# Two plain blocks per FFN in place of four, and weight splits and sinks' exponentials moved in ScalarE's queue

## The chip, the cores and the metric

The kernel runs on one core of a Trainium2 chip. The core has five engines that work side by side: TensorE (PE in the profile; PEld is its weight load), VectorE (DVE), ScalarE (ACT), GpSimd (POOL) and SyncE (SP), which here only issues DMAs. Each takes its instructions in the order in which the compiled program has them. The metric is the device time of one execution in microseconds; lower is better. The time of the kernel before is the median of three runs.

## The reference

What is computed is a decoder trunk of two layers over 512 tokens of width 1024. Each layer is a half-step gated FFN, a mixer, a second half-step FFN and a final norm.

```python
def swiglu(x, w1, w3, w2):
    return (jax.nn.silu(x @ w1) * (x @ w3)) @ w2
...
    for l in range(DEPTH):
        h = x + 0.5 * swiglu(rms_norm(x, ffn1_norm[l]), ffn1_w1[l], ffn1_w3[l], ffn1_w2[l])

        n = rms_norm(h, mix_norm[l])
        p = n @ w_in[l]
        u_conv, q, k, v, q_mem = jnp.split(p, splits, axis=-1)

        y_conv = conv_module(u_conv, conv_w[l], conv_b[l], conv_ln_g[l], conv_ln_b[l])
...
        y_swa = sliding_window_attention(q, k, v, swa_sinks[l])
...
        y_mem = memory_attention(qm, mk, mv)

        y = jnp.concatenate([y_conv, y_swa, y_mem], axis=-1)
        h = h + y @ w_out[l]

        h = h + 0.5 * swiglu(rms_norm(h, ffn2_norm[l]), ffn2_w1[l], ffn2_w3[l], ffn2_w2[l])

        x = rms_norm(h, final_norm[l])
```

The hidden width of an FFN is 2816, 22 blocks of 128. The mixer has 384 channels of a causal depthwise convolution with 31 taps, six heads of attention in a window of 128 with a learned sink each, and four heads that attend to 256 memory tokens. All of it is in float32.

## The kernel before, in words

Every float32 operand of a matmul is split into a rounded high part and a low part that holds the rest (`split`, lines 144 to 146): ScalarE writes the high part, VectorE the low one. A product is then three matmuls, high by high, low by high, high by low (`mm3`, lines 175 to 178). Weights arrive by a DMA into a `raw` tile, of which there are three, and are split into one of four pairs `whi`, `wlo`. For some weights the low part is made without VectorE: ScalarE writes the high part and the negated high part's source (lines 150 and 151), and a DMA on GpSimd's queue adds the weights to it in place (line 152, `split_by_dma`).

**The FFN** (line 405 on). Tokens are in the columns, and x is the residual h times the norm's gain; the factor R of the norm, one per token, comes later, from column sums of squares (`sums`), a small matmul that spreads it over all partitions (`spread`) and a copy by ScalarE. The first four blocks of the hidden width are "plain" (`PLAIN`, line 269): two projections (w1 and w3) of 24 matmuls with 512 columns for each block, run on x, and after that `gate` multiplies by R, applies silu and splits the result. While they run, VectorE makes n = h times gain times R (`normed`) and the operands of a scheme that needs seven products in place of eight for a pair of blocks (`Seven`): `first` makes operands 1, 2 and 6 (`mh`, `ml`), `rest` makes 3, 5, 7 and 4, in the tiles of x, which come free with the last plain projection. From there on `up_pair` (line 341) does two blocks at a time: 14 products of 12 matmuls with 256 columns for both w1 and w3. It splits seven weight tiles on ScalarE and VectorE (`unit`); some of them are sums of two blocks' weights, which DMAs (line 349) and VectorE (line 369) add up. Four quarters of the hidden width follow one another, and at the end of each one w2 is applied and added into h (line 475).

In the layer-1 first FFN, h must also be scaled by the final norm of layer 0 (`after`, line 1050). This is eight VectorE instructions (line 1053), queued behind the first seven-product pair.

How many projections come before the column sums and the spread is given by `at_product`: two and one for the first FFN of a layer, one and one for the second. So behind R there are in the first FFN one, in the second two of the first four projections.

**The mixer** (line 623 on). At the end of an FFN `last(d)` calls `Next`, which rounds the new operand `xhi` on ScalarE (line 155), takes the rest on VectorE (line 156) and squares h on ScalarE (line 236) for the column sums. Then `ORDER` (line 47) says in which order the mixer's steps are written: c are halves of convolution projections, q and Q query and key projections and their transposes, v and V value and memory-query projections and their transposes, g the scores of an attention group, a the rest of the attention, t the conv taps of a channel block, s the conv's norm and the output projection. The four query weight tiles (`queries`, line 693) are split ahead of the first q; three of them by `split_by_dma`.

The conv's taps are 30 VectorE instructions for each of three channel blocks after a first one (lines 932 and 939). `EARLY` of them go freely, and `LATER` deals the others out over the attention groups: a tap may only come after the softmax step `biased` of its group.

In attention (line 861 on), ScalarE makes the exponentials of scores (`powers`, line 800) and copies transposed ones out of PSUM (line 812), TensorE multiplies them with the values (line 821), and `scaled` adds the exponential of the sink (line 829) to the sums. Its argument `esw` comes from GpSimd (line 791). Output weights (`out_weights`, line 920 on) are split by ScalarE and a DMA; two before the attention and two in the midst of it.

The compiler schedules: it orders the instructions of each engine by the order in which they are written and by when it expects them to be ready. `tc.issue_after(i)` adds an edge: what its block writes on the engine of `i` stands behind `i` in that engine's queue. `queued()` is this with the last matmul.

Of the kernel before, what the change touches and what calls it, by code (L numbers as in the profile page):

```python
# [46 lines left out]
ORDER = "c00 c01 q0 c10 q1 c11 Q0 q2 q3 Q1 c20 c21 Q2 v0 v1 V0 Q3 V1 g0 g1 v2 v3 a t0 t1 t2 s"  # L47

EARLY = 49
LATER = (1, 12, 5, 4, 3, 3, 3, 3, 3, 3)  # L50
# [14 lines left out]
def trunk(ctx: ExitStack, tc: tile.TileContext, xT, memT, pos, w1a, w3a, w2a, w1b, w3b, w2b,  # L65
# [88 lines left out]
    def split_scaled(hi, lo, x, col):  # L154
        A.activation(hi, x, AF.Copy, scale=col)
        V.scalar_tensor_tensor(out=lo, in0=x, scalar=col, in1=hi.bitcast(F32), op0=ALU.mult, op1=ALU.subtract)

# [95 lines left out]
    class Next:  # L253
# [5 lines left out]
        def __call__(self, d):  # L259
            split_scaled(self.x[0][:, d, :], self.x[1][:, d, :], h[:, d, :], self.gain[:, d : d + 1])  # L260
            for s, scale in self.stats:
                s.add(h[:, d, :], 1.0 if scale is None else scale[:, d : d + 1])
# [78 lines left out]
    def up_pair(l, w13, f, M):  # L341
# [26 lines left out]
        def add(out, a, b):  # L368
            V.tensor_tensor(out=out, in0=a, in1=b, op=ALU.add)  # L369
# [15 lines left out]
        for i in range(2):  # L385
            w = unit(X[i])
            product(xy[i][:, x0], w, 1, 5)
            A.activation(part[i][:, x0], xy[i][:, x0], AF.Copy)
            product(zv[i][:, x1], w, 0, 7)
            add(to[i][:, :, x1], zv[i].rearrange("p (n t) -> p n t", n=2), part[i][:, x0].unsqueeze(1).to_broadcast([P, 2, QT]))  # L390
# [14 lines left out]
    def ffn(l, w13, w2, x, sums, factors, last, at_product, aside=None):  # L405
# [14 lines left out]

        g, products = {}, []
        for f in range(0, PLAIN, 2):
            g[f], g[f + 1] = gated()
# [16 lines left out]
        with queued():  # L440
            for f in range(0, PLAIN, 2):
                u, v = (tmp.tile([P, 2, S], F32, tag=t, name=t, bufs=n) for t, n in (("u", 1), ("g", 2)))
                for j in range(2):
                    while len(products) < 2 * (f + j) + 2:
                        products.append(up(len(products) // 2, len(products) % 2))
                    gate(products[2 * (f + j) :], R, u[:, j], v[:, j], *g[f + j])
                if not f:
                    M.first()
        M.rest()
        for q, (f0, nf) in enumerate(QUARTERS):  # L450
            ahead = 2 if q + 1 < len(QUARTERS) else 0
            for f in range(f0, f0 + nf + ahead, 2):
                if f not in g:
                    g[f], g[f + 1] = up_pair(l, w13, f, M)
                    if f == PLAIN:
                        with tc.issue_after(M.gated.ins):
                            after()
# [86 lines left out]

    def head_scale(ps, col, n, out=None):

        sq = tm("hsq", "sq", 2)[:, 0 : n * HD]
        A.activation(sq, ps, AF.Square, scale=col)
# [74 lines left out]
    def mixer(l, x, st, last):  # L623
# [69 lines left out]
        def queries(t):  # L693
            if not t:
                ww["q"] = [weights(wqk[l, i], 1024, G if i else V, spare()) for i in range(4)]
# [30 lines left out]
        def values(t):  # L726
# [9 lines left out]
            head_scale(ps[:, 0:256], rc[:, t : t + 1], NM, rm[:, t, :])  # L736

# [85 lines left out]
        def scaled(kind, b, po):  # L823
# [3 lines left out]
            if kind == "w":  # L827
                e = esw[:, b]
                A.activation(e, e, AF.Exp)
# [31 lines left out]
        def attention():  # L861
# [18 lines left out]
            for d in range(2):  # L880
                with tc.issue_after(keyed[2].ins):
                    out_weights(d)
            yy.extend([gated_pair() for _ in range(KD // 2)][::-1])
            y.extend(at(p, ALL, i, ALL) for p in yy for i in range(2))
            for n, (kind, *pairs) in enumerate(GROUPS):
# [8 lines left out]
                if n in (3, 5):  # L894
                    with tc.issue_after(raised[GROUPS[n - 1][0], *GROUPS[n - 1][-1]].ins):
                        out_weights(len(out_w))
# [108 lines left out]
    def stages(st, gain):  # L1005
        def factors(r):
            return gain, kept(spread(r), "R"), lambda: None
# [3 lines left out]
    for l in range(L):  # L1011
# [16 lines left out]
        mixer(l, nxt.x, before, into(gn[:, l, N_FFN2], (st, None)))  # L1028
        sums, factors = stages(st, gn[:, l, N_FFN2])
        st, fin = Stat("st"), gn[:, l, N_FIN]  # L1030
        if l + 1 < L:
# [15 lines left out]
            def factors(r, gg=gg, fin=fin):  # L1047
                R = kept(spread(r[1]), "R")

                def after():  # L1050
                    RF = kept(spread(r[0]), "RL")
                    for d in range(KD):
# [70 lines left out]
```

## Time and profile before

| | |
|---|---|
| time, median of 3 runs (lowest to highest) | 1791.13 us (1789.97 to 1793.52) |
| the profiled execution's own time | 1790.99 us |
| its span | 1789.2 us |
| mean granted TensorE clock | 0.994 |
| TensorE busy | 1757.0 us (98%) |
| VectorE busy | 1272.3 us (71%) |
| ScalarE busy | 899.4 us (50%) |
| GpSimd busy | 194.4 us (11%) |
| DMA | 253.32 MB, mean 142 GB/s |

The span runs from the first to the last instruction of the profiled execution; 1.8 us of its time lie outside. In a row of the timeline stand the start in us, the duration in us, the engine, the line of the kernel, the operation, what it writes and reads by the program's names, and the count; in square brackets the idle time of the engine ahead of it and what ended it. Matmuls overlap: one of 512 columns has a duration of 0.39 us, but the next one starts sooner, so the distance of starts is what a matmul costs. Line 176 is the high-by-high matmul of a product, 177 low by high, 178 high by low.

### The profile page before, as it was taken

The numbers are of one execution on the slowest core, as the hardware profiler recorded it, in microseconds if no ns is written. First come the engines' busy times: TensorE is split into PE (matmuls) and PEld (weight loads), VectorE is DVE, ScalarE is ACT, GpSimd is POOL, SyncE is SP. The second block draws the span as 40 slices with busy tenths as digits, with TensorE's granted clock in tenths as the row PEclk, the third lists the DMA queues.
The fourth block names the chain that finished last, engine by engine and source line by source line (L and its number), as shares of the span: only waits on it lengthen the run. The fifth ranks groups of instructions, "written<-read, shape, count | busy, mean of one in ns | idle before, by whom it ended". The sixth has DMA issues, their size and how long they took to land.

```text
span 1789.2 us, 28081 instructions
## 1 busy us (share of the span) xinstructions
PE 1757.0 (98%) x11004; PEld 1581.5 (88%) x11004; DVE 1272.3 (71%) x1887; ACT 899.4 (50%) x1367; POOL 194.4 (11%) x217
## 2 busy tenths in 40 slices
PE   8999999999999999999999999999999999999997
PEld 6989999878788989898889898989787889998986
DVE  6969666589947857575678685756797567666755
ACT  6646444464765535353655453535455655453532
POOL 1001000034221000000010000000441210000000
PEclk9999999999999999999999999999999999999998
DMA  9456555183167547464656474643631966574622
GB/s 280 125 163 177 165 139 145 57 217 70 30 176 172 139 136 177 127 173 128 165 136 170 131 190 135 169 114 105 158 70 30 234 127 171 136 183 119 168 74 82
DMA packets 95892, 253.32 MB, mean 142 GB/s; under 512 B 9872, under 2 KB 14224, under 8 KB 95760
## 3 DMA queue, kind: packets, MB, share of 16 engines
q1 hardware_dynamic: 77040, 190.45, 34.9%
q0 software_dynamic: 18720, 61.09, 19.3%
q8 instruction: 86, 1.41, 0.3%
q14 instruction: 46, 0.38, 0.1%
HBM read 249.40 MB, written 2.10 MB: 141 GB/s over the span
## 4 chain that ended last, share of the span: by engine, by line
PE 81%; issue 6%; DVE 6%; DMA 4%; ACT 3%; POOL 0%; SPq 0%; POOLq 0%; DVEq 0%; ACTq 0%
PE mm L177 12%; PE mm L176 11%; PE mm L178 11%; PE po L176 8%; PE po L178 8%; PE po L177 8%; PE pt L176 6%; PE pt L177 6%; PE pt L178 6%; DVE there L939 2%; DMA glo<-in_wqk 1%; DMA raw<-in_wout 1%; DVE wlo L146 1%; PE cf L178 1%; PE cf L176 1%
## 5 line engine op out<-in xcount | busy, mean ns | idle before, releaser
L145 ACT ACTIVATE whi<-raw 128x1024 fp32r<-128x1024 f32 (+3 forms) x344 | 324.5, 945 | 440.5 <-PE mm L177 223.5
L146 DVE TENSOR_TENSOR wlo<-raw,whi 128x1024 fp32r<-128x1024 f32 (+3 forms) x344 | 372.0, 1083 | 133.9 <-ACT whi L145 132.6
L177 PE MATMUL mm<-glo,whi 128*128 128x512 f32 x752 | 293.3, 390 | 0.8 <-DVE glo L146 0.8
L176 PE MATMUL mm<-ghi,whi 128*128 128x512 f32 x752 | 293.3, 392 | 0.0
L178 PE MATMUL mm<-ghi,wlo 128*128 128x512 f32 x734 | 285.7, 389 | 0.9 <-DVE wlo L146 0.9
L177 PE MATMUL po<-ml,whi 128*128 128x256 f32 x864 | 244.5, 283 | 0.0
L178 PE MATMUL po<-mh,wlo 128*128 128x256 f32 x864 | 244.5, 283 | 0.0
L176 PE MATMUL po<-mh,whi 128*128 128x256 f32 x864 | 244.4, 283 | 0.0
L176 PE MATMUL pt<-xhi,whi 128*128 128x256 f32 x864 | 243.3, 283 | 0.6 <-DVE g L369 0.6
L178 PE MATMUL pt<-xhi,wlo 128*128 128x256 f32 x864 | 243.9, 283 | 0.0
L177 PE MATMUL pt<-xlo,whi 128*128 128x256 f32 x864 | 243.9, 283 | 0.0
L475 DVE SCALAR_TENSOR_TENSOR h<-mm,h 128x512 f32<-128x512 f32 x128 | 87.8, 689 | 133.3 <-PE mm L178 133.3
L177 PEld LDWEIGHTS mm<-glo,whi 128*128 128x128 f32 x752 | 141.3, 188 | 29.9 <-DVE glo L146 1.6
L176 PEld LDWEIGHTS mm<-ghi,whi 128*128 128x128 f32 x752 | 141.3, 188 | 29.4 <-DVE h L475 1.2
L176 PEld LDWEIGHTS pt<-xhi,whi 128*128 128x128 f32 x864 | 165.2, 192 | 1.7 <-DVE g L369 0.8
L177 PEld LDWEIGHTS pt<-xlo,whi 128*128 128x128 f32 x864 | 165.7, 192 | 0.8
L176 PEld LDWEIGHTS po<-mh,whi 128*128 128x128 f32 x864 | 165.8, 192 | 0.7
L177 PEld LDWEIGHTS po<-ml,whi 128*128 128x128 f32 x864 | 165.8, 192 | 0.6
L178 PEld LDWEIGHTS po<-mh,wlo 128*128 128x128 f32 x864 | 165.8, 192 | 0.0
L178 PEld LDWEIGHTS pt<-xhi,wlo 128*128 128x128 f32 x864 | 165.6, 192 | 0.0
L178 PEld LDWEIGHTS mm<-ghi,wlo 128*128 128x128 f32 x734 | 137.8, 188 | 30.2 <-DVE wlo L146 1.3
L939 DVE SCALAR_TENSOR_TENSOR there<-ypad,par,there 128x512 f32<-128x512 f32 x180 | 136.7, 770 | 1.6
(312 smaller groups left out, 3312.9 us busy)
## 6 DMA issues: line engine op xcount, KB each, us to landing
raw<-in_w2a SPq DMA_DIRECT2D x48, 384.0 KB, 3.5
raw<-in_w2b SPq DMA_DIRECT2D x48, 384.0 KB, 3.6
raw<-in_w1b SPq DMA_DIRECT2D x26, 512.0 KB, 3.7
raw<-in_w3b SPq DMA_DIRECT2D x26, 512.0 KB, 4.1
raw<-in_w1a SPq DMA_DIRECT2D x25, 512.0 KB, 3.7
raw<-in_w3a SPq DMA_DIRECT2D x25, 512.0 KB, 3.8
wsum<-in_w1a SPq DMA_DIRECT2D x18, 512.0 KB, 4.5
wsum<-in_w3a SPq DMA_DIRECT2D x18, 512.0 KB, 4.4
```

The lines of the kernel that those rows point to most:

```text
L145: A.activation(hi, x, AF.Copy)
L146: on.tensor_tensor(out=lo, in0=x, in1=hi.bitcast(F32), op=ALU.subtract)
L176: T.matmul(ps, a[0], b[0], start=first, stop=False, **more)
L177: T.matmul(ps, a[0], b[1], start=False, stop=False, **more)
L178: tail[0] = T.matmul(ps, a[1], b[0], start=False, stop=last, **more)
L475: added = V.scalar_tensor_tensor(out=h[:, d, :], in0=ps, scalar=0.5, in1=h[:, d, :], op0=ALU.mult, op1=ALU.add)
L939: V.scalar_tensor_tensor(out=cv[:, c, :], in0=ypad[:, c, j : j + S], scalar=conv_w[:, c, j : j + 1], in1=cv[:, c, :], op0=ALU.mult, op1=AL ...
```

## The change

`plain` is 4 in the program's first FFN and 2 in the three others. There the third and fourth block are done by `up_pair`, and the final scaling of h in the layer-1 FFN comes in two halves, the first behind the first seven-product pair, the second within the next pair. In the mixer three of the four query weight splits are queued behind the last rounding of x; the third block of values (v2) is written ahead of the first scores; the output weights are split in steps v0 and v2 and no longer in the attention; the sink's exponential is queued behind the last exponentials of its block's scores; and `EARLY` and `LATER` are dealt anew.

```diff
-ORDER = "c00 c01 q0 c10 q1 c11 Q0 q2 q3 Q1 c20 c21 Q2 v0 v1 V0 Q3 V1 g0 g1 v2 v3 a t0 t1 t2 s"
-
-EARLY = 49
-LATER = (1, 12, 5, 4, 3, 3, 3, 3, 3, 3)
+ORDER = "c00 c01 q0 c10 q1 c11 Q0 q2 q3 Q1 c20 c21 Q2 v0 v1 V0 Q3 v2 g0 V1 g1 v3 a t0 t1 t2 s"
+
+EARLY = 55
+LATER = (1, 12, 5, 4, 3, 3, 3, 3, 2, 2)
...
-            split_scaled(self.x[0][:, d, :], self.x[1][:, d, :], h[:, d, :], self.gain[:, d : d + 1])
+            self.rounded = split_scaled(self.x[0][:, d, :], self.x[1][:, d, :], h[:, d, :], self.gain[:, d : d + 1])
...
+        plain = PLAIN if first else 2
         g, products = {}, []
-        for f in range(0, PLAIN, 2):
+        for f in range(0, plain, 2):
             g[f], g[f + 1] = gated()
...
-            for f in range(0, PLAIN, 2):
+            for f in range(0, plain, 2):
...
-                    if f == PLAIN:
-                        with tc.issue_after(M.gated.ins):
-                            after()
+                    if f in (plain, plain + 2):
+                        with tc.issue_after((M.gated if f == plain else M.turned).ins):
+                            after(f > plain)
...
             if not t:
-                ww["q"] = [weights(wqk[l, i], 1024, G if i else V, spare()) for i in range(4)]
+                ww["q"] = []
+                for i in range(4):
+
+                    with tc.issue_after(operand.rounded.ins) if i else nullcontext():
+                        ww["q"].append(weights(wqk[l, i], 1024, G if i else V, spare()))
...
+            for d in {0: (0, 1, 2), 2: (3,)}.get(t, ()):
+                with tc.issue_after((squared[-1] if d > 1 else keyed[2]).ins):
+                    out_weights(d)
...
-                A.activation(e, e, AF.Exp)
+                with tc.issue_after(raised[kind, b, CC - 1].ins):
+                    A.activation(e, e, AF.Exp)
...
-            for d in range(2):
-                with tc.issue_after(keyed[2].ins):
-                    out_weights(d)
...
-                if n in (3, 5):
-                    with tc.issue_after(raised[GROUPS[n - 1][0], *GROUPS[n - 1][-1]].ins):
-                        out_weights(len(out_w))
...
-                def after():
-                    RF = kept(spread(r[0]), "RL")
-                    for d in range(KD):
+                def after(half):
+                    if not half:
+                        spreads.append(kept(spread(r[0]), "RL"))
+                    RF = spreads[0]
+                    for d in range(4 * half, 4 * half + 4):
                         V.scalar_tensor_tensor(out=h[:, d, :], in0=h[:, d, :], scalar=fin[:, d : d + 1], in1=RF, op0=ALU.mult, op1=ALU.mult)
```

`M.turned` is the last addition that takes the sixth and seventh product's results out of PSUM (line 390), `squared[-1]` the latest square for a head's norm (line 548), `keyed[2]` the copy of the third block of keys (line 720), `first` a list that the program's first FFN empties.

More of the change, by code (lines that the diff above doesn't have):

```diff
@@ L154, in split_scaled @@
     def split_scaled(hi, lo, x, col):
-        A.activation(hi, x, AF.Copy, scale=col)
+        rounded = A.activation(hi, x, AF.Copy, scale=col)
         V.scalar_tensor_tensor(out=lo, in0=x, scalar=col, in1=hi.bitcast(F32), op0=ALU.mult, op1=ALU.subtract)
+        return rounded
     def pair():
@@ L368, in add @@
         def add(out, a, b):
-            V.tensor_tensor(out=out, in0=a, in1=b, op=ALU.add)
+            return V.tensor_tensor(out=out, in0=a, in1=b, op=ALU.add)
         for i in range(2):
@@ L389, in up_pair @@
             product(zv[i][:, x1], w, 0, 7)
-            add(to[i][:, :, x1], zv[i].rearrange("p (n t) -> p n t", n=2), part[i][:, x0].unsqueeze(1).to_broadcast([P, 2, QT]))
+            M.turned = add(to[i][:, :, x1], zv[i].rearrange("p (n t) -> p n t", n=2), part[i][:, x0].unsqueeze(1).to_broadcast([P, 2, QT]))
         w = unit(z)
@@ L543, in heads @@
         return x.rearrange("p (h e) -> p h e", e=HD)
+    squared = []
     def head_scale(ps, col, n, out=None):
         sq = tm("hsq", "sq", 2)[:, 0 : n * HD]
-        A.activation(sq, ps, AF.Square, scale=col)
+        squared.append(A.activation(sq, ps, AF.Square, scale=col))
         ss, v = sm(n, f"hs{n}"), sm(n, f"hv{n}")
@@ L621, in prepare, with mixer @@
         memory(l)
-    def mixer(l, x, st, last):
+    def mixer(l, operand, st, last):
+        x = operand.x
         o = CC * TAPS
@@ L1006, in factors @@
         def factors(r):
-            return gain, kept(spread(r), "R"), lambda: None
+            return gain, kept(spread(r), "R"), lambda half: None
         return lambda: rms_cols(st, D), factors
@@ L1027, in trunk @@
         before, st = st, Stat("st")
-        mixer(l, nxt.x, before, into(gn[:, l, N_FFN2], (st, None)))
+        mixer(l, nxt, before, into(gn[:, l, N_FFN2], (st, None)))
         sums, factors = stages(st, gn[:, l, N_FFN2])
@@ L1047, in factors @@
             def factors(r, gg=gg, fin=fin):
-                R = kept(spread(r[1]), "R")
-                def after():
-                    RF = kept(spread(r[0]), "RL")
-                    for d in range(KD):
+                R, spreads = kept(spread(r[1]), "R"), []
+                def after(half):
[3 more added lines that the diff above has]
+                    for d in range(4 * half, 4 * half + 4):
                         V.scalar_tensor_tensor(out=h[:, d, :], in0=h[:, d, :], scalar=fin[:, d : d + 1], in1=RF, op0=ALU.mult, op1=ALU.mult)
```

## The prediction

> **What bounds the kernel now.** I read the page first (busy shares and the chain that ended last), then the busy time of each engine in the stretches that the change touches, then the timelines of those stretches.
>
> ```profile
> span 1789.2 us, 28081 instructions
> ...
> PE 1757.0 (98%) x11004; PEld 1581.5 (88%) x11004; DVE 1272.3 (71%) x1887; ACT 899.4 (50%) x1367; POOL 194.4 (11%) x217
> ...
> PE 81%; issue 6%; DVE 6%; DMA 4%; ACT 3%; POOL 0%; SPq 0%; POOLq 0%; DVEq 0%; ACTq 0%
> ```
>
> TensorE is busy for 98% of the span and makes 81% of the chain. So time is won in two ways only: fewer or shorter matmuls, or one of the few waits of TensorE taken away. Everything else counts only where it makes TensorE wait. The profiled execution took 1790.99 us for its span of 1789.2 us; the median of the runs is 1791.13 us, 0.14 us more, so I sum against the profiled execution and carry the result over unchanged.
>
> The next view is the busy time by engine in six stretches (us, then PE, PEld, DVE, ACT, POOL busy, the granted clock, DMA share, GB/s).
>
> ```profile
> 556.50:587.60 31.10, 31.10 (x139) 25.76 (x138) 26.61 (x39) 14.62 (x20) 2.43 (x3) 1.00 0.57 122
> 910.20:935.80 25.60, 25.60 (x114) 21.21 (x113) 25.53 (x38) 12.52 (x17) 1.49 (x2) 1.00 0.45 100
> ...
> 370.00:390.00 20.00, 19.09 (x90) 14.98 (x89) 12.12 (x20) 13.62 (x17) 5.85 (x6) 1.00 0.89 241
> 430.00:440.00 10.00, 9.19 (x60) 8.62 (x61) 8.98 (x17) 5.34 (x14) 4.32 (x4) 1.00 0.67 133
> ...
> 455.00:460.00 5.00, 3.17 (x30) 2.77 (x27) 4.97 (x10) 4.06 (x12) 2.19 (x4) 1.00 0.00 0
> 460.00:465.00 5.00, 5.00 (x28) 3.46 (x27) 3.99 (x8) 2.50 (x8) 0.91 (x2) 0.66 0.74 131
> ```
>
> The first two rows run, in the second FFN of layer 0 and the first FFN of layer 1, from the moment the row factor R is there to the first matmul of the seven-product scheme. TensorE has no gap in either. VectorE is busy for 26.61 of 31.10 us in the one and 25.53 of 25.60 us in the other: in the layer-1 FFN it is already full under the cover of the plain blocks. The other rows are in the mixer of layer 0. At 455 to 460 us TensorE works only 3.17 of 5 us, and in the 5 us after that its granted clock is 0.66.
>
> **Part 1: two plain blocks in three FFNs.** Four projections of 24 matmuls, 512 columns wide, are replaced by 14 products of 12 matmuls, 256 wide. Their price is the distance between starts on TensorE's timeline.
>
> ```profile
> 571.32 0.39 PE L176 MATMUL mm<-xhi,whi 128*128 128x512 f32 x1
> ...
> 587.63 0.28 PE L176 MATMUL po<-mh,whi 128*128 128x256 f32 x1
> ...
> 593.39 0.40 PE L176 MATMUL pt<-xhi,whi 128*128 128x256 f32 x2
> ```
>
> Three projections (72 matmuls by the code) lie between the first two rows: 16.31/72 = 0.2265 us each. Four products (48) lie between the second and third: 5.76/48 = 0.120 us each. The removed work is 96 x 0.2265 = 21.74 us, the added work 168 x 0.120 = 20.16 us: 1.58 us less per FFN, 4.7 us in three.
>
> [...]
>
> VectorE does not shrink in step. What goes are the eight instructions of two gates; what comes is the work of one more pair. The cover in front of the first seven-product matmul falls by 21.7 us. So here is when VectorE delivers, first in the layer-1 FFN, then in the second FFN of layer 0:
>
> ```profile
> 910.18 5.39 DVE L275 SCALAR_TENSOR_TENSOR n<-h,gg,R 128x512 f32<-128x512 f32 x8 [5.79 <-ACT R L221]
> ...
> 917.28 1.28 DVE L146 TENSOR_TENSOR ml<-n,mh 128x512 fp32r<-128x512 f32 x2
> ...
> 920.28 1.29 DVE L146 TENSOR_TENSOR ml<-n,mh 128x512 fp32r<-128x512 f32 x2
> ...
> 923.29 1.22 DVE L146 TENSOR_TENSOR wlo<-raw,whi 128x1024 fp32r<-128x1024 f32 x1
> ...
> 925.03 0.69 DVE L415 TENSOR_TENSOR u<-po,R 128x512 f32<-128x512 f32 x1
> ...
> 926.83 0.69 DVE L369 TENSOR_TENSOR raw<-raw,wsum 128x512 f32<-128x512 f32 x1
> 927.44 1.22 DVE L146 TENSOR_TENSOR wlo<-raw,whi 128x1024 fp32r<-128x1024 f32 x1
> 928.57 1.22 DVE L146 TENSOR_TENSOR ml<-msum,mh 128x1024 fp32r<-128x1024 f32 x1
> ```
> ```profile
> 556.56 5.39 DVE L275 SCALAR_TENSOR_TENSOR n<-h,gn,R 128x512 f32<-128x512 f32 x8 [7.74 <-ACT R L221]
> ...
> 566.07 1.29 DVE L146 TENSOR_TENSOR ml<-n,mh 128x512 fp32r<-128x512 f32 x2
> ...
> 572.12 1.22 DVE L146 TENSOR_TENSOR ml<-msum,mh 128x1024 fp32r<-128x1024 f32 x1
> ```
> ```profile
> 908.49 0.48 PE L176 MATMUL po<-xhi,whi 128*128 128x512 f32 x1
> ```
>
> The last row is the start of the last of the first four projections in the layer-1 FFN; it ends 24 x 0.2265 = 5.4 us later, at 913.9. In the new kernel the products that need the first `ml` pair are next. I assume that VectorE keeps its order up to there: eight `n`, gates, first `ml` pair (done at 918.56), second pair (921.57), the summed one (929.79). Two things bring these forward. R's copy no longer has the weight split of a third block ahead of it on ScalarE: 0.9 us. And four of the rows above (923.29, 925.03, 926.83, 927.44: 1.1 + 0.6 + 0.6 + 1.1 = 3.4 us by their starts) fall away or can lie in the 5.79 us that VectorE idles before R. Then the first `ml` pair is there at 917.7: TensorE waits 3.7 us. The second is there at 920.7, and TensorE wants it at 917.7 + 12 x 0.12 = 919.1: 1.6 us. The summed one is there at 925.5, wanted at 920.7 + 36 x 0.12 = 925.0: 0.4 us. Together 5.7 us. A wait of that length also lowers the clock: after the hole at 455 to 460 the 5 us at 0.66 lost up to 1.7 us, and I add 1.0. What comes after (the remaining sums, five more weight splits) I take as covered by the first two products of the next pair, whose operands exist by then: 0. Bounds: 0 if the order is better than before, and above as in the second rival.
>
> [...]
>
> In the second FFN of either layer one more projection lies behind R. The four projections end at 565.9 (571.32, where a sixth begins, less the 24 x 0.2265 of the fifth), the second `ml` pair is done at 567.36 less 0.9, in time, and the summed one at 573.34 less 0.9 less 0.6 (`u` of the third block), 571.8, wanted at 565.9 + 5.8 = 571.7. So nothing is late by more than a few tenths; I take 1.0 us each for the work behind it. Sum of the FFNs: -4.7 + 6.7 + 2 x 1.0 = +4.0 us.
>
> The final scaling of h moves too: eight VectorE instructions now come in two halves behind two different pairs. In the kernel before they stand ahead of a weight split that TensorE waits for:
>
> ```profile
> 976.11 0.50 PE L178 MATMUL mm<-ghi,wlo 128*128 128x512 f32 x1 [0.89 <-DVE wlo L146]
> ```
>
> That goes: -0.9 us, once. FFNs: +3.1 us.
>
> **Part 2: three weight splits behind the last rounding (each mixer).** ScalarE's order at the mixer's start, and TensorE beside it:
>
> ```profile
> 370.05 0.71 ACT L155 ACTIVATE xhi<-h,gn 128x512 fp32r<-128x512 f32 x1
> ...
> 371.21 1.06 ACT L150 ACTIVATE ghi<-raw 128x1024 fp32r<-128x1024 f32 x1
> ...
> 373.12 0.70 ACT L155 ACTIVATE xhi<-h,gn 128x512 fp32r<-128x512 f32 x1
> ...
> 375.20 1.04 ACT L151 ACTIVATE glo<-raw 128x1024 fp32r<-128x1024 f32 x1
> ```
> ```profile
> 373.88 0.50 PE L176 MATMUL mm<-xhi,whi 128*128 128x512 f32 x1 [0.46 <-ACT xhi L155]
> 374.67 0.50 PE L177 MATMUL mm<-xlo,whi 128*128 128x512 f32 x1 [0.28 <-DVE xlo L156]
> ```
> ```profile
> 376.54 10.70 DMA glo<-in_wqk
> ```
>
> TensorE starts these two at 0.8 us distance instead of 0.23, so about 1.2 us go when the last `xhi` comes at about 371.2: -1.2. But the splits are moved past it with their DMAs: three pairs of about 2.0 us from 372.5 on end at 378.6 and not 376.2, the accumulating DMA on POOL's queue follows 2.4 us later, and the chain has this one, 10.70 us long, as the query weights' last. With TensorE 1.2 us earlier, the wait for it could grow by 3.6 us. Against that, the DMA engines are 0.89 busy in this stretch, and while the raw buffers wait for ScalarE the next weight loads on SP's queue cannot start beside it. Between 0 and 3.6 I take 1.5.
>
> **Part 3: attention.** One more block of value columns before the first scores, output weights split earlier, sinks' exponential later.
>
> ```profile
> 438.04 0.44 PE L581 MATMUL pt<-cst,aux 128*128 128x128 f32 x2 [0.81 <-ACT there L583]
> ```
> ```profile
> 456.64 0.21 ACT L829 ACTIVATE esw<-esw 128x6 f32<-128x6 f32 x1 [0.94 <-POOL esw L791]
> 456.76 0.79 ACT L800 ACTIVATE uu<-mm,nmw,rq 128x128 f32<-128x128 f32 x2
> 457.44 0.73 ACT L150 ACTIVATE whi<-raw 128x640 fp32r<-128x640 f32 x1
> 458.07 0.59 ACT L812 ACTIVATE aux<-pt 128x512 f32<-128x512 f32 x1
> ```
> ```profile
> 458.71 0.99 PE L821 MATMUL po<-mvn,aux 128*128 128x65 f32 x7 [1.83 <-ACT aux L812]
> ...
> 469.58 0.66 PE L810 MATMUL pt<-cst,uu 128*128 128x128 f32 x4 [0.69 <-ACT aux L812]
> ```
>
> The first wait gets 24 matmuls of the third block of values put in front of it: -0.8. Ahead of the copy at 458.07 that TensorE waits for stand 0.94 of waiting for POOL, 0.12 of exponential and 0.63 of a weight split, 1.7 us, which all go. With the hole goes the clock's fall: up to 1.7 us (5 x 0.34), I take 1.2. The wait of 0.69 stands behind another such split: -0.7. That is 3.6 us; but VectorE is busy for 4.97 of 5 us there and sets part of the pace itself, so I take 3.0 (from 0 to 3.6). The earlier splits cost nothing: ScalarE is busy for 5.34 of 10 us at 430 to 440, and without that room they would cost two instructions of 0.63 us each, twice; their loads on SP's queue and accumulating DMAs on POOL's go up with them, into a stretch where the DMA engines are 0.67 busy. The sinks' exponential now stands behind the block's last exponentials of scores; only VectorE's sum of the denominators waits for it, and that comes after the block's last product anyway. The conv taps are only dealt out anew.
>
> Each mixer: -1.2 + 1.5 - 0.8 - 3.0 = -3.5 us; two: -7.0. Sum of all: +3.1 - 7.0 = -3.9 us, so 1790.99 - 3.9 = 1787.1 us.
>
> **The rivals.** First, the query weights are as late as they can be (3.6 us) and attention follows VectorE (1.0 us gained): each mixer then gives +0.6 us, the whole +3.1 + 1.2 = +4.3: 1795.3. For it speaks the long DMA on the chain; against it that half of that stretch's traffic moves away. This one is slower by little.
>
> Second, slower: VectorE becomes the bound of the change-over in all three FFNs. It has 25.53 - 8 x 0.6 = 20.7 us of work in the second row of the table of stretches, and TensorE only 913.9 - 909.3 = 4.6 us of cover; about 5.8 us (three splits, four sums) can be done before R. That makes up to 10.3 us of wait, and by the same count 26.61 - 4.8 - 10.2 - 5.8 = 5.8 us in each of the others. At two thirds of that, with the clock's fall, 8.6 + 2 x 3.9 = 16.4 against my 8.7 us: 1794.8; at the full bound 1802. From 12.6 us of waits in the three together the change gains nothing, from 16.2 us it can be measured as slower. For it: VectorE has no slack in the layer-1 FFN. Against it: 4.5 us of slack in the others, and VectorE's order can put what TensorE needs first.
>
> Third, better: the compiled order has the first products' operands ready (3.7 us wait in the layer-1 FFN, none elsewhere) and the mixers gain all (-1.2 - 0.8 - 3.6, no late weights: -11.2): -4.7 + 3.7 - 0.9 - 11.2 = -13.1, so 1777.9.
>
> Fourth, the plain count does not change because the list that decides it is not empty after the first FFN: then only the mixers count, 1784.0. By the code it is emptied there.
>
> **How the numbers follow.** About 0.2%, 3.6 us, is what a measurement can tell from no change. My forecast has 0.45, and its own range is 1782 to 1791 (the mixers' -11 to -3 around the FFNs' +3, with a little for the waits); some 0.6 of it lies below 1787.5. First rival 0.15, second 0.20, third 0.17, fourth 0.03. Faster: 0.45 x 0.6 + 0.17 + 0.03 = 0.47; slower: 0.20 x 0.7 + 0.15 x 0.65 = 0.24; the rest, 0.29, is within. The range reaches from just above the third to just above the second: 1779 to 1797.
>
> **What would show it.** Right: 504 more matmuls of 128x256 and 288 fewer of 128x512; a wait of TensorE for `ml` or `mh` near the layer-1 FFN's start; the wait for `aux` at L821 gone, and the clock at 1.00 after it; the last `xhi` ahead of the three query splits. Wrong: no such wait for `ml` (third rival), waits of over 16 us in the three FFNs (second), or a longer wait for `glo<-in_wqk` (first).

## The result, and the profile after

The changed kernel takes 1819.33 us (median of four runs, 1817.01 to 1823.34) against 1792.33 us for the kernel before on the same chip (median of four). That is 27.0 us more by the medians; the ratio with its 95% interval is 1.0158 (1.0143 to 1.0173), which makes 28 us. 1787.1 us was predicted, and the range ended at 1797.

The page of the changed kernel, the lines that were shown of the kernel before (span; busy time; the chain that ended last). The profiled execution is the slowest of the four, 1823.34 us. In this kernel, and in those made from it, the three matmuls of a product are lines 177 to 179, one further on than before:

```profile
span 1821.6 us, 28578 instructions
...
PE 1768.4 (97%) x11220; PEld 1597.5 (88%) x11220; DVE 1300.3 (71%) x1923; ACT 904.7 (50%) x1382; POOL 192.9 (11%) x211
...
PE 74%; issue 11%; DVE 9%; DMA 3%; ACT 2%; POOL 0%; SPq 0%; POOLq 0%; DVEq 0%; ACTq 0%
```

TensorE's busy time grew although its work shrank: at a lower clock a matmul counts as longer (one of 256 columns 0.41 us and not 0.28, in the 5 us from 590 on, where the granted clock is 0.59). Its part of the chain fell from 81% to 74%, and VectorE's rose from 6% to 9%. The page hardly shows more: over the whole span VectorE is busy for 71%, as before. The list of TensorE's waits shows more (what waits, for what; us in total, times, longest):

```profile
...
PE cf L203 <- DVE st L249: 5.1, 2, 2.5
PE po L178 <- DVE ml L146: 4.7, 6, 1.8
PE po L177 <- ACT xhi L145: 4.1, 2, 2.0
PE po L178 <- DVE xlo L146: 3.0, 2, 1.5
...
PE mm L782 <- ACT there L587: 2.5, 2, 1.3
```

None of these pairs stood in the list of the kernel before. `ml`, `xhi` and `xlo` at L145 and L146 are operands of the seven products: the three FFNs. `st` is the sum of squares at a mixer's start, `there` a copy in attention.

To place the loss I add up, from the starts of the matmuls in the trace, by how much each distance exceeds the usual one for its width (0.227 us at 512 columns, 0.120 at 256). This counts the waits and the slower matmuls behind them. The kernel before loses 36.6 us in this way, the changed one 74.0: 37.4 more, less 4.7 of saved matmul work makes 32.7, and the spans differ by 32.4. By place: second FFN of layer 0, 10.2 us (before 0); first FFN of layer 1, 14.9 (before 1.7); second FFN of layer 1, 9.3 (before 0.9); the two mixers together 32.0 (before 27.1).

**The FFNs.** Busy time by engine in stretches of the changed kernel (us, then PE, PEld, DVE, ACT, POOL, granted clock, DMA share, GB/s); below it one row of the kernel before that the prediction didn't read, its first seven-product pair:

```profile
558.50:601.00 42.50, 36.52 (x228) 33.12 (x228) 41.44 (x57) 22.09 (x31) 1.78 (x2) 0.92 0.36 89
...
590.00:595.00 5.00, 5.00 (x28) 5.00 (x28) 4.74 (x10) 1.96 (x4) 0.00 (x0) 0.59 0.87 201
...
912.00:963.00 51.00, 43.13 (x262) 39.78 (x261) 44.44 (x65) 22.61 (x32) 4.74 (x4) 0.87 0.29 75
```
```profile
587.60:610.00 22.40, 22.40 (x188) 22.36 (x187) 21.50 (x28) 14.47 (x20) 1.73 (x2) 1.00 0.61 143
```

In the second FFN of layer 0 (first row) VectorE works 41.44 of 42.5 us: it is the bound from R's arrival to the end of the first pair. And in the kernel before it was already busy for 21.50 of the 22.40 us of the first pair, behind a cover in which it worked 26.61 of 31.10. The third row is the first FFN of layer 1, where the granted clock is 0.87 over 51 us. VectorE's timeline in the second FFN of layer 0, the ScalarE row that leads to it, and TensorE's waits:

```profile
557.40 1.06 ACT L145 ACTIVATE whi<-raw 128x1024 fp32r<-128x1024 f32 x1 [5.34 <-PE mm L178]
```
```profile
558.49 1.23 DVE L146 TENSOR_TENSOR wlo<-raw,whi 128x1024 fp32r<-128x1024 f32 x1 [3.71 <-PE pt L216]
559.63 5.38 DVE L276 SCALAR_TENSOR_TENSOR n<-h,gn,R 128x512 f32<-128x512 f32 x8
...
579.77 1.21 DVE L146 TENSOR_TENSOR ml<-msum,mh 128x1024 fp32r<-128x1024 f32 x1
...
582.98 2.48 DVE L305 TENSOR_TENSOR msum<-n 128x512 f32<-128x512 f32 x4
585.39 2.34 DVE L146 TENSOR_TENSOR wlo<-raw,whi 128x1024 fp32r<-128x1024 f32 x2
587.66 2.35 DVE L146 TENSOR_TENSOR xlo<-msum,xhi 128x1024 fp32r<-128x1024 f32 x2
```
```profile
574.02 0.39 PE L177 MATMUL po<-mh,whi 128*128 128x256 f32 x1 [0.95 <-DVE g L418]
...
581.03 0.39 PE L178 MATMUL po<-ml,whi 128*128 128x256 f32 x1 [0.69 <-DVE ml L146]
...
585.95 0.39 PE L177 MATMUL po<-xhi,whi 128*128 128x256 f32 x1 [2.03 <-ACT xhi L145]
...
588.92 0.58 PE L178 MATMUL po<-xlo,whi 128*128 128x256 f32 x1 [1.51 <-DVE xlo L146]
```

The second weight split could not lie ahead of R, since its tile came free only with a projection at 557.4: VectorE idled 3.71 us and then did it ahead of `n`. The summed `ml` pair is done 21.35 us after `n` begins, where the kernel before took 16.78: gates, weight splits and sums now lie between. The wait of 2.03 us is put down to ScalarE's `xhi`, but what that rounds are the sums that VectorE makes only from 582.98 on. Behind the waits the clock falls to 0.59. The second FFN of layer 1 shows the same: the summed `ml` pair 21.35 us after `n` begins, and the same waits within 0.02 us.

In the first FFN of layer 1 a weight split goes ahead of something small that all waits for, the mean square `ms`:

```profile
912.54 1.22 DVE L146 TENSOR_TENSOR wlo<-raw,whi 128x1024 fp32r<-128x1024 f32 x1 [1.17 <-ACT whi L145]
913.68 0.15 DVE L209 TENSOR_SCALAR ms<-cf 128x4 f32<-128x4 f32 x1
```
```profile
913.89 1.05 PE L203 MATMUL cf<-onesq,RL 128*128 128x1 f32 x8 [1.01 <-DVE ms L209]
...
930.44 0.50 PE L177 MATMUL pt<-xhi,whi 128*128 128x256 f32 x2 [1.85 <-ACT xhi L145]
931.99 0.55 PE L178 MATMUL po<-ml,whi 128*128 128x256 f32 x1 [1.05 <-DVE ml L146]
...
944.18 0.50 PE L177 MATMUL po<-mh,whi 128*128 128x256 f32 x2 [2.14 <-ACT mh L145]
946.50 0.58 PE L178 MATMUL po<-ml,whi 128*128 128x256 f32 x1 [1.81 <-DVE ml L146]
```

The last of these rows waits for the summed `ml` pair, which is done 22.3 us after `n` begins (924.15 to 946.44); behind it TensorE waits no more in this FFN. Here is each FFN's loss, waits and slower matmuls together, in three parts (the sums differ by up to 0.2 us from those above, by where the stretch is cut):

| lost by TensorE (us) | ahead of R | from R to the summed `ml` | behind it |
|---|---|---|---|
| second FFN of layer 0 | 0.2 | 2.9 | 7.3 |
| first FFN of layer 1 | 2.9 | 9.3 | 2.7 |
| second FFN of layer 1 | 0.1 | 3.0 | 6.4 |

Of the 34.4 us in the three, waits make 20 us and the slower matmuls behind them nearly all of the rest.

**The mixers.** ScalarE, then TensorE, at the start of layer 0's, and in attention:

```profile
370.97 0.74 ACT L155 ACTIVATE xhi<-h,gn 128x512 fp32r<-128x512 f32 x1
371.60 1.04 ACT L150 ACTIVATE ghi<-raw 128x1024 fp32r<-128x1024 f32 x1
...
374.44 1.04 ACT L151 ACTIVATE glo<-raw 128x1024 fp32r<-128x1024 f32 x1
375.39 0.61 ACT L237 ACTIVATE sq<-h 128x512 f32<-128x512 f32 x1
...
446.00 0.74 ACT L150 ACTIVATE whi<-raw 128x640 fp32r<-128x640 f32 x1
...
447.25 0.39 ACT L587 ACTIVATE there<-pt 128x256 f32<-128x256 f32 x1
```
```profile
376.78 1.05 PE L203 MATMUL cf<-onesq,st 128*128 128x1 f32 x8 [2.53 <-DVE st L249]
...
447.69 0.48 PE L782 MATMUL mm<-mT,there 64*128 64x256 f32 x1 [1.27 <-ACT there L587]
...
462.29 1.11 PE L834 MATMUL po<-mvn,aux 128*128 128x65 f32 x8 [1.15 <-ACT aux L825]
```

The last rounding is early as intended (370.97, before 373.12). But a rounding is followed by a square, and four copies of split weights slipped in between the two: the column sums start at 376.78 and not at 375.27, and in the 5 us from 380 on the granted clock is 0.75. The longest wait for the query weights (`glo<-in_wqk`) is 0.58 us here, before 0.2. In attention the split of the fourth output weight stands ahead of a copy; the wait removed (0.81) has become one of 1.27.

### The profile page after: what moved, and what is told of

It is laid out like the page before. It is cut to its first block, busy times and chain, and to the rows that moved or that the text cites. A ratio compares the mean times of both kernels' runs of the same rounds, so it can differ in the third digit from the quotient of the medians.

```text
span 1821.6 us, 28578 instructions
## 1 busy us (share of the span) xinstructions
PE 1768.4 (97%) x11220; PEld 1597.5 (88%) x11220; DVE 1300.3 (71%) x1923; ACT 904.7 (50%) x1382; POOL 192.9 (11%) x211
## 3 DMA queue, kind: packets, MB, share of 16 engines
q1 hardware_dynamic: 78672, 192.02, 34.4%
## 4 chain that ended last, share of the span: by engine, by line
PE 74%; issue 11%; DVE 9%; DMA 3%; ACT 2%; POOL 0%; SPq 0%; POOLq 0%; DVEq 0%; ACTq 0%
PE mm L178 10%; PE mm L177 10%; PE mm L179 10%; PE po L178 8%; PE po L179 8%; PE po L177 8%; PE pt L178 5%; PE pt L179 5%; PE pt L177 5%; DVE there L947 2%; DVE wlo L146 1%; DMA glo<-in_wqk 1%; DVE n L276 1%; PE cf L177 1%; PE cf L179 1%
## 5 line engine op out<-in xcount | busy, mean ns | idle before, releaser
L145 ACT ACTIVATE whi<-raw 128x1024 fp32r<-128x1024 f32 (+2 forms) x359 | 340.1, 950 | 458.9 <-PE mm L178 239.8
L146 DVE TENSOR_TENSOR wlo<-raw,whi 128x1024 fp32r<-128x1024 f32 (+2 forms) x359 | 389.7, 1087 | 137.0 <-ACT whi L145 125.2
L178 PE MATMUL po<-ml,whi 128*128 128x256 f32 x936 | 267.3, 286 | 4.7 <-DVE ml L146 4.7
L177 PE MATMUL po<-mh,whi 128*128 128x256 f32 x936 | 266.3, 285 | 4.0 <-ACT mh L145 2.1
L177 PE MATMUL pt<-xhi,whi 128*128 128x256 f32 x936 | 264.8, 284 | 3.0 <-ACT xhi L145 3.0
L179 PE MATMUL po<-mh,wlo 128*128 128x256 f32 x936 | 266.3, 285 | 0.0
L179 PE MATMUL pt<-xhi,wlo 128*128 128x256 f32 x936 | 265.3, 284 | 0.0
L178 PE MATMUL pt<-xlo,whi 128*128 128x256 f32 x936 | 265.2, 284 | 0.0
L178 PEld LDWEIGHTS po<-ml,whi 128*128 128x128 f32 x936 | 181.3, 194 | 6.8 <-DVE ml L146 5.9
L179 PEld LDWEIGHTS po<-mh,wlo 128*128 128x128 f32 x936 | 181.3, 194 | 0.0
```

Of the source, the lines that this page charges most:

```text
L145: A.activation(hi, x, AF.Copy)
L146: on.tensor_tensor(out=lo, in0=x, in1=hi.bitcast(F32), op=ALU.subtract)
L177: T.matmul(ps, a[0], b[0], start=first, stop=False, **more)
L178: T.matmul(ps, a[0], b[1], start=False, stop=False, **more)
L179: tail[0] = T.matmul(ps, a[1], b[0], start=False, stop=last, **more)
```

## The experiments

Theory 1: in the FFNs VectorE's queue is the bound, so each microsecond of its work that goes from the change-over comes back. Rivals: the fourth projection's PSUM bank (the wait for `g` above); ScalarE and the buffers. For the mixers: the late query splits (by the square, or by the weights themselves) against attention. All kernels, each against the kernel before on the same chip:

| kernel | median us | ratio [95% interval] |
|---|---|---|
| FFN part alone | 1818.58 | 1.0158 [1.0135, 1.0180] |
| two plain blocks in second FFNs alone | 1806.22 | 1.0087 [1.0071, 1.0104] |
| changed, other bank | 1820.25 | 1.0172 [1.0152, 1.0192] |
| and gates behind the first pair | 1814.26 | 1.0145 [1.0121, 1.0170] |
| and splits by DMA, three FFNs | 1837.07 | 1.0251 [1.0234, 1.0267] |
| the same in second FFNs alone | 1815.36 | 1.0128 [1.0110, 1.0147] |
| changed, gates' VectorE work left out | 1804.34 | 1.0079 [1.0066, 1.0093] |
| and operand sums left out | 1796.10 | 1.0032 [1.0020, 1.0045] |
| mixer part alone | 1796.11 | 1.0029 [1.0017, 1.0041] |
| query splits back | 1789.26 | 0.9984 [0.9975, 0.9993] |
| two query splits behind the square | 1790.31 | 0.9994 [0.9985, 1.0003] |
| three query splits behind the square | 1796.72 | 1.0031 [1.0021, 1.0042] |
| query splits back, fourth output weight later | 1794.84 | 1.0018 [1.0008, 1.0029] |
| sinks' exponential alone | 1791.03 | 1.0002 [0.9992, 1.0012] |
| query splits back, without the exponential | 1788.66 | 0.9992 [0.9983, 1.0002] |

**FFN part alone** (the mixers' hunks of the diff taken back).

> The FFN part alone (two plain blocks in three FFNs, final scaling in halves); the mixers are those of the kernel before. Theory 1, VectorE's queue sets the pace of the change-over: TensorE's lost time in the three FFNs of the changed kernel is 10.2 + 14.9 + 9.3 = 34.4 us against 1.8 before, less 4.7 of matmul work: about +28 us over the kernel before, near 1820. The prediction's own count of this part was +3.1 us (near 1795). If this kernel is much below 1815, the loss in the FFNs is one that only the two parts together make.

The FFN part alone costs what the whole change costs; theory 1's count holds. The two parts by themselves (27.6 and 5.1 us) add up to more than the 27.0 us of the whole, all by medians; in the profiled executions the whole is 32.4. The intervals of the two large ratios span 5 and 8 us, and no run settles this difference.

**Two plain blocks in the second FFNs alone** (on the kernel before; the other hunks carry `plain` through, as in the change).

```diff
+        plain = 2 if w13[0] is w1b else PLAIN
```

> The kernel before with two plain blocks in the two second FFNs alone; the layer-1 first FFN keeps four, mixers as before. Theory 1, each FFN's loss is its own (VectorE's queue against its own cover): 10.2 + 9.3 us of lost time less 2 x 1.6 us of matmul work, +16 us, so 1806 to 1809. The prediction's count: 2 x (1.0 - 1.6) = -1 us, 1790. Rival, most of the loss comes from the first of the three FFNs in a chain (late weights carried on): under 1800.

16 us for two FFNs whose matmuls save 3.2: about 9.5 us of loss each, where 1.0 was predicted. So each FFN's loss is its own; of the FFN part's 27.6 us some 12 are left for the first FFN of layer 1.

**The fourth projection's bank** (on the changed kernel, as are the next two).

```diff
-            ps = bank([P, S], "po" if 2 * f + i in (3, 4) else "mm")
+            ps = bank([P, S], ("cf" if plain == 2 else "po") if 2 * f + i in (3, 4) else "mm")
```

> The changed kernel, with the fourth projection of the three FFNs in the bank of the column sums and no longer in one of the two that the first seven-product pair needs. Theory 2, the bank is what makes TensorE wait: the waits for g at the first pair (1.9 us by the list of waits, about 1 us in each second FFN) go and the pair starts earlier, -2 to -4 us. Theory 1, VectorE's queue is the bound: whatever TensorE gains there it waits for at the next operand, within 1 us of the changed kernel.

The wait for `g` is gone, the time is not; in the second FFN of layer 0 TensorE now has two longer waits:

```profile
578.80 0.50 PE L177 MATMUL po<-mh,whi 128*128 128x256 f32 x2 [1.70 <-ACT mh L145]
...
582.69 0.38 PE L178 MATMUL po<-ml,whi 128*128 128x256 f32 x1 [2.21 <-DVE ml L146]
```

Freeing the bank moved the wait and did not remove it: the bank is not the cause.

**Gates behind the first pair** (with the other bank).

```diff
             for f in range(0, plain, 2):
+                if plain == 2:
+                    while len(products) < 4:
+                        products.append(up(len(products) // 2, len(products) % 2))
+                    M.first()
+                    continue
...
                     g[f], g[f + 1] = up_pair(l, w13, f, M)
+                    if f == plain == 2:
+                        with tc.issue_after(M.gated.ins):
+                            u, v = (tmp.tile([P, 2, S], F32, tag=t, name=t, bufs=n) for t, n in (("u", 1), ("g", 2)))
+                            for j in range(2):
+                                gate(products[2 * j :], R, u[:, j], v[:, j], *g[j])
```

> As the kernel with the fourth projection in the column sums' bank, and in the three FFNs the gates of the two plain blocks (16 VectorE and ScalarE steps, of which 8 on VectorE at 0.6 us each) are written behind the first seven-product pair. Nothing is left out. Theory 1, VectorE's queue is the bound: 4.8 us of VectorE's work less ahead of the operands in each of three FFNs, -14 us, and up to 5 us more where the clock fell after the longer waits: 1800 to 1806. Theory 2, the bank alone: no more than the kernel with only the bank moved. Theory 3, the row factor and the units' splits ahead of it make the loss: the gates' place changes under 4 us.

Against the kernel with the other bank alone 6.0 us go by the medians (5 by the ratios, 8.4 by the profiled spans, 1817.8 and 1809.4), with runs from 1811.2 to 1818.3. No theory's number came out; the next view shows what took part of the gain back: first the change-over, then the pair that now has the gates in it:

```profile
556.60:594.50 37.90, 35.32 (x233) 32.60 (x232) 36.73 (x49) 19.97 (x28) 1.78 (x2) 0.95 0.39 100
594.50:611.50 17.00, 15.70 (x131) 15.49 (x130) 16.72 (x24) 10.86 (x18) 1.72 (x2) 1.00 0.64 180
```

VectorE is nearly full in both, 36.73 of 37.9 and 16.72 of 17.0 us: the pair that takes the gates has no room for them.

**Splits by DMA**, in the first two pairs of the three FFNs, then of the second FFNs alone (there on the kernel before):

```diff
-    def unit(x):
+    def unit(x, src=()):
         p = pair()
+        if src:
+            A.activation(p[0], x, AF.Copy)
+            A.activation(p[1], x, AF.Copy, scale=-1.0)
+            for c, w in src:
+                G.dma_start(p[1][:, c], w, accum_op=ALU.add)
+            return p
...
-            w = unit(raw[i])
+            w = unit(raw[i], [(blk(0, UNIT), w13[i][l, f])] if light else ())
...
-        w = unit(z)
+        w = unit(z, [(blk(i, QW), w13[i][l, f + 1, :, QW:]) for i in range(2)] if light else ())
```

> As the changed kernel with the gates behind the first pair and the fourth projection in the column sums' bank; besides, in the first two seven-product pairs of the three FFNs three of seven weight tiles get their low part by an accumulating DMA and not by VectorE. Nothing is left out. Theory 1, VectorE's queue is the bound: 3 x 1.14 us less VectorE work in each of the two pairs, 6.8 us per FFN, of which some 3 to 5 come back in time as long as TensorE still waits: 1800 to 1806 against 1814. Rival, DMA or ScalarE takes its place (each such tile costs ScalarE 1.04 us more and a transfer of 512 KB): no better than 1812.

> The kernel before with two plain blocks in the two second FFNs alone, where the cover behind the row factor is one projection longer, with the gates behind the first pair and three of seven weight tiles of the first two pairs split by DMA. Theory 1, VectorE's queue is the bound: in these FFNs the traces show 4.4 to 5.3 us of lost time left with late gates; 6.8 us less VectorE work each takes most of it away and the 1.6 us of saved matmuls each come through: 1788 to 1793, about the kernel before. Rival, ScalarE or DMA becomes the bound: 1796 or more.

Both rivals hold: the first kernel is 23 us slower than with late gates alone, the second 7 (by the ratios) to 9 us (by the medians) slower than two plain blocks in the second FFNs without any relief. TensorE's waits in the second of these kernels:

```profile
580.11 0.79 PE L176 MATMUL pt<-xhi,whi 128*128 128x256 f32 x2 [2.38 <-ACT xhi L145]
593.04 0.39 PE L178 MATMUL pt<-xhi,wlo 128*128 128x256 f32 x1 [1.92 <-DMA wlo<-in_w1b]
```

The four accumulating transfers issued from 585 to 592 us need 6.4 to 8.1 us each, and they start only when ScalarE has written the negated copy. VectorE's work is relieved, but TensorE waits for the transfers instead.

**Work left out**, so that nothing takes its place:

```diff
+            if self.bare:
+                return self.plain(6, 0, 1)
...
+            if self.bare:
+                for j in (5, 7, 4):
+                    self.plain(j, 0, 1)
+                return
...
         def gate(pp, R, u, g, hi, lo):
+            if plain == 2:
+                A.activation(hi, pp[1], AF.Copy)
+                A.activation(lo, pp[0], AF.Silu)
+                return
```

The first kernel has the hunk of `gate` alone, the second all three.

> The changed kernel with part of the work left out: in the three FFNs with two plain blocks, their gates write two ScalarE results and do none of VectorE's eight steps (8 x 0.6 = 4.8 us in each FFN); ScalarE loses its copies too. Everything else, matmuls and transfers too, is kept. Theory 1, VectorE's queue is the bound: 3 x 4.8 = 14 us less, and more where the clock stays up: 1800 to 1806. Rival, ScalarE's order and the buffers of weights make the waits: under 5 us less.

> As the kernel without the gates' VectorE work, and besides the twelve sums of 0.6 us each that make four of the seven products' operands are left out in the same three FFNs (plain quarters are split in their place): in all 12 us of VectorE's work less in each. Theory 1, VectorE's queue is the bound: 36 us less work against 34.4 us of lost time, so nearly all of the loss goes: 1786 to 1793, with 1 to 3 us of single waits left in each FFN. Rival, as before: over 1810.

14.4 us less VectorE work gives 14 us by the ratios (15.0 by the medians, with kernels before that differ by 1.0); 36 us less gives 22 to 23, of the 28 that the FFN part costs (the last forecast missed by 3 us: it forgot the mixers' 5 us, and some waits stay). With both left out (second FFN of layer 0, then first of layer 1):

```profile
557.00:600.00 43.00, 42.72 (x310) 40.46 (x309) 35.11 (x48) 28.02 (x45) 1.79 (x2) 1.00 0.41 111
908.00:960.00 52.00, 48.60 (x343) 45.31 (x342) 37.96 (x57) 29.88 (x48) 3.21 (x4) 0.96 0.41 111
```
```profile
904.68 1.44 PE L203 MATMUL cf<-onesq,RL 128*128 128x1 f32 x8 [1.02 <-DVE ms L209]
```

In the first TensorE works nearly throughout and the loss is 0.5 us. In the second 9 of 14.9 us stay although VectorE has room: half of it is the wait for `ms` (last row) and the slower matmuls behind it (granted clock 0.52 in the 5 us from 905 on), where the order of VectorE's queue counts and not its amount; the other half is three waits of 0.47 to 1.38 us, one of them for the copies that stand in for the gates. Holding back the weight split ahead of `ms` was not tried.

**Mixer part alone** (four plain blocks, final scaling in one piece).

> The mixer part alone (query weight splits, order of steps, output weights, sinks' exponential, taps); four plain blocks and the final scaling in one piece behind the first pair as before. From TensorE's lost time in the two traces the mixers should cost +4.8 us together, so near 1797. The prediction had -7.0 us (near 1785). If the late query splits are the whole cost, the loss sits ahead of the second convolution half and nowhere later.

1796.11 us, as counted from the traces: the mixer part by itself costs 5.1 us where 7.0 were to be gained.

**Query splits back**: `issue_after(operand.rounded.ins)` taken away.

> The mixer part alone, but the four query weight splits are where the kernel before has them. Theory 1, the late splits are the cost of the mixer part: five ScalarE copies of about 1 us each stand ahead of the last square of h, so the column sums come 1.5 us later and the clock falls behind that hole; in the trace of the mixer part alone this stretch loses 6.3 us against 1.9 in the first mixer. Undone, the kernel falls by 6 to 8 us from 1796, to 1788 to 1790. Theory 2, attention is what costs (the fourth output weight's split ahead of a copy that TensorE waits for): it stays within 2 us of 1796.

Theory 1 holds (four copies, not five, stand ahead of the square): 6.9 us go by the medians (8 by the ratios), and what is left of the mixer part is faster than the kernel before by 2.4 us by the medians; the interval is 1.3 to 4.5 us. Of all kernels here it alone is measurably faster.

**Query splits behind the last square**, two of them (`i > 1`, shown) and then three (`i`), on the mixer part alone; `squared` is the latest square of h.

```diff
-                    with tc.issue_after(operand.rounded.ins) if i else nullcontext():
+                    with tc.issue_after(operand.stats[0][0].squared.ins) if i > 1 else nullcontext():
```

> The mixer part alone, with the last two of the four query weight splits behind the last square of h and the second one where it was before. Theory: the hole in front of the column sums came from the split copies ahead of the last square; here none stands there, and the last rounding isn't late either. Against the kernel with the query splits back (1789.3) the 1.2 us of the late rounding go in each mixer: 1786 to 1789. Rival: the later query weights make TensorE wait by as much: 1789 to 1792.

> The mixer part alone, with three query weight splits behind the last square and not behind the last rounding. If the square was all that the late splits cost, the column sums come 2.9 us earlier than in the changed kernel and the clock stays up: 1786 to 1790. If the weights themselves are late too (the first rival of the prediction), the wait moves to the first query product, 3 to 4 us in each mixer, and it stays at 1792 to 1796.

With three behind it the square is in time and the hole is gone, but the weights are late, by 3.95 us in the first mixer:

```profile
387.94 0.50 PE L178 MATMUL mm<-glo,xhi 128*128 128x512 f32 x1 [1.81 <-DMA glo<-in_wqk]
...
391.74 0.50 PE L178 MATMUL mm<-glo,xhi 128*128 128x512 f32 x1 [2.14 <-DMA glo<-in_wqk]
```

So the late splits cost either way: the square, or else the query weights. With two behind it one such wait stays, 1.63 us in the first mixer, and at 1790.31 us the gain is gone: the rival's range. With three the time, 1796.72, lies 0.7 us above the range that was given for late weights.

**Fourth output weight behind the copy** (on the kernel with the query splits back).

> As the kernel with the query weight splits back, and the fourth output weight is split behind the copy of the second block of memory queries out of PSUM and no longer ahead of it. Theory: that split's two ScalarE steps, 0.63 us each, made the wait of 1.44 us that took the place of the one removed; without them it falls to 0.2 or less in each mixer: 2 to 3 us less than the kernel with the query splits back alone, and so 2 to 4 us under the kernel before. Rival: VectorE sets the pace of attention and the gain is caught by the next wait: within 1 us.

Both expectations missed: 5.6 us slower. The wait aimed at shrank (its idle time was 1.28 us), the next grew:

```profile
444.68 0.48 PE L788 MATMUL mm<-mT,there 64*128 64x256 f32 x1 [0.47 <-ACT there L590]
...
460.09 1.11 PE L840 MATMUL po<-mvn,aux 128*128 128x65 f32 x8 [1.52 <-ACT aux L831]
```

The later wait, 1.19 in the kernel with the query splits back, is now 1.52, and behind it the granted clock is 0.69 (1.00 in the other kernel):

```profile
460.00:465.00 5.00, 4.91 (x27) 3.44 (x28) 4.70 (x11) 2.90 (x8) 1.52 (x2) 0.69 0.00 0
```

By the traces TensorE loses 2.5 us more in all, and the two profiled spans differ by 2.4 us; the profiled execution of this kernel took 2.7 us less than the median of its runs. Why the other runs take longer stays open.

**Exponential alone, and all but the exponential.**

> The kernel before with the sink's exponential alone queued behind the last exponentials of its block's scores. Theory A, the 0.94 us in which ScalarE waits for GpSimd's sum ahead of the copy is on TensorE's path: the wait of 1.83 us falls by about 1 us in each mixer, and the clock, which fell to 0.66 behind that hole, stays up: -2 to -6 us, 1786 to 1789. Theory B, VectorE sets the pace there, or the weight split alone holds the copy: within 1 us of the kernel before.

> The mixer part with the query weight splits back, and the sink's exponential where the kernel before has it: so the earlier third block of values, the earlier output weights and the new dealing of taps alone. Theory A, the exponential makes the gain: 1790 to 1793, no gain over the kernel before. Theory B, the moved output weights make it: 1788 to 1790, as the kernel that has the exponential too.

Alone it gives nothing, as theory B has it: the interval is 1.4 us below to 2.1 us above. Yet in its trace the wait of 1.83 us is 0.71, and the one of 0.69 behind it has become 1.40:

```profile
457.55 1.11 PE L821 MATMUL po<-mvn,aux 128*128 128x65 f32 x8 [0.71 <-ACT aux L812]
...
467.91 0.66 PE L810 MATMUL pt<-cst,uu 128*128 128x128 f32 x4 [1.40 <-ACT aux L812]
```

Without it the rest of the mixer part takes 1788.66 us, in the range of theory B. But the kernels with and without it (0.9984 and 0.9992) have overlapping intervals, so which piece makes the 2.4 us stays open.

## Why the prediction was wrong

**Matmul count, right.** 504 narrow ones more and 288 wide ones fewer make 216, and the page counts 11220 against 11004.

**FFN waits, wrong, and this decided the sign.** The prediction had 5.7 us of waits, 1.0 of clock and 2 x 1.0 us, 8.7 in all; the trace has 14.9, 10.2 and 9.3, 34.4 in all. The mechanism, VectorE delivering the operands late, was the prediction's own; its steps on how late failed:

- "I assume that VectorE keeps its order up to there", and that four rows "fall away or can lie in the 5.79 us that VectorE idles before R". The third block's `u` fell away and two splits and four sums came ahead of R, but the next split's weight tile was not free, so it landed ahead of `n`, and gates and more splits lay ahead of the summed `ml` pair. By the prediction's count that pair was done 16.2 us after `n` begins (909.3 to 925.5); in the first FFN of layer 1 it took 22.3. From R to there TensorE lost 9.3 us in the first FFN of layer 1, against 5.7 and 1.0. In the second FFNs, where "nothing is late by more than a few tenths", it lost 3 us each.
- "What comes after (the remaining sums, five more weight splits) I take as covered by the first two products of the next pair ...: 0", and 1.0 us in each second FFN. It cost 2.7 us in the one and 7.3 and 6.4 in the others. The first pair had VectorE at 21.50 of 22.40 us already; it could cover nothing.
- What lay ahead of R was not in the sum: the split that went ahead of `ms`, 2.9 us in the first FFN of layer 1.

The slower matmuls are in these numbers. The forecast had one fall of the clock, 1.0 us; it fell behind most of the longer waits (to 0.59 in the 5 us from 590 on, 0.66 from 915, 0.71 from 930, 0.57 from 945), and all of this makes some 14 us. The runs with work left out show that in the second FFNs VectorE's amount of work is the cause. In the first FFN of layer 1 it is part of it; that the order ahead of `ms` makes some 3 to 4.5 us is read from the traces and not tested.

The second rival had this mechanism as the bound, with 0.20. Its 10.3 + 2 x 5.8 = 21.9 us were too low for the same reason: it counted VectorE's work up to the first matmul of the pair and let the pair itself pass as free.

**Final scaling, right.** The wait of 0.89 us at 976 is gone.

**Query splits, wrong.** -1.2 + 1.5 was forecast for a mixer. The rounding came when the step said, but the last square stands behind it on the same engine and was not counted: the wait ahead of the column sums is 2.53 us, the clock falls to 0.75 behind it (the 5 us from 380 on), and taken back the move gives 6.9 us in two mixers. The first rival's 3.6 us of late weights did not show in the changed kernel (a wait of 0.58 us), since the square was late first; the run with the square in time has 3.95.

**Attention, the mechanism right, the size wrong.** The wait at L821 fell from 1.83 to 1.15 us, and the clock held (1.00 from 460 to 470). But 0.81 came back as 1.27, put there by an output weight split that was forecast to cost nothing, "ScalarE is busy for 5.34 of 10 us at 430 to 440": the fourth split stands at 446, not there. Forecast -3.8 us for each mixer, measured without the late query splits -1.2.

## What to carry to other kernels

When cover is taken away from an engine, count that engine's work over the whole stretch until it next has slack, not up to the first operand: the pair behind the cover was already full. Count the slower matmuls behind a wait with it: here 20 us of waits came to 34. A wait seen in one place is worth its size only if the queue behind it has room. And when a step is put "behind the last X", look for what followed X on that engine, here a square of 0.6 us that all of the next stage waited for.

## What the runs showed of the hardware

In the runs the granted clock did not follow from the length of a wait alone. In one kernel (query splits back, without the exponential) the same wait occurs in both mixers; here TensorE's rows, and the 5 us behind each:

```profile
458.57 1.11 PE L835 MATMUL po<-mvn,aux 128*128 128x65 f32 x8 [1.14 <-ACT aux L826]
```
```profile
1340.06 1.10 PE L835 MATMUL po<-mvn,aux 128*128 128x65 f32 x8 [1.15 <-ACT aux L826]
```
```profile
460.00:465.00 5.00, 5.00 (x38) 3.72 (x38) 4.96 (x14) 3.79 (x9) 0.71 (x1) 1.00 0.00 0
...
1340.00:1345.00 5.00, 4.94 (x26) 3.88 (x26) 4.08 (x10) 2.87 (x8) 0.90 (x2) 0.66 0.00 0
```

After equal waits the clock is 1.00 once and 0.66 once. The 5 us with the wait in them look alike too: TensorE was busy for 3.86 of the 5 us from 455 on and for 3.92 of the 5 us from 1335 on. What decides between them no row here shows. By an estimate from these rows, what a wait cost differed by up to 1.7 us (5 x 0.34) between two like places of one kernel.
